# Quadrant moves of a transposed hidden tile, cut into four steps and a split and spread over the next pair of weight chunks

## The chip, the cores and the metric

The kernel runs on one core of one Trainium2 chip. The metric is the device time of one execution in microseconds (us), from start to end of the program on that core; lower is better. Three timed runs of the kernel before lie within 0.07% of each other.

## The reference, cut to what matters

A two-layer decoder trunk over 256 tokens of width 2048: attention, a SwiGLU feed-forward and a gated embedding in each layer. The change lies in the feed-forward:

```python
def swiglu(h, w1, w3, w2):
    return (jax.nn.silu(h @ w1) * (h @ w3)) @ w2      # D_MODEL = 2048, D_FF = 5632, SEQ = 256
```

Everything is float32.

## The kernel before, in words

**Products.** A float32 product is made of three TensorE products of a rounded format. Every operand is split into a high half (`hi`, a rounding copy on ScalarE, line 130 for weights and line 311 for activations) and a low half (`lo`, the difference, on VectorE, line 131 or 312). Lines 391, 392 and 393 multiply hi by hi, lo by hi and hi by lo into the same accumulator. All matmuls of the feed-forward are 128 x 128 by 128 x 512.

**Weight stream.** `WeightStream` loads blocks of four 128-row tiles by 512 columns (1 MB) from HBM, three raw buffers deep, and splits them up to three blocks ahead of their use, into three pairs of half buffers. A split therefore waits until TensorE has finished the block whose half buffer it takes over.

**A pair of chunks.** The hidden width is 11 chunks of 512 columns, in groups of 3, 4 and 4. For a chunk, `pair_of_chunks` makes the products with `w1` and `w3` together. The first four 128-row tiles of the contraction go through a seven-product form (Winograd's variant of Strassen), in which sums of weight tiles and of activation tiles are multiplied. Its small blocks live in three held tiles, `r11`, `r12` and `r2`; their halves `shi` and `slo` have a single buffer each, so a small split waits until TensorE is through with the small block before. In program order a pair is twelve blocks: small block 0 (`r11`, product `p1`, 6 matmuls), 1 (24 matmuls), small 2 (`r12`, `p7`, 6), 3 (24), small 4 (`r11`, `p5`, 6), 5 (24), 6 (`r2`, 12), 7 (24), small 8 (`r11`, `p6`, 6), 9 (24), small 10 (`r11`, 6), 11 (24): 186 matmuls. The weight sums (line 121) stand at the head of the split that reads them: block 2 first forms `r11 += r12` and `r12 += r2[1]`, block 8 `r11 += r2[1]`, block 10 `r11 += r2[0]`.

**End of a pair.** `feed_forward` takes the four accumulators, forms the hidden tile on VectorE and ScalarE (lines 619 to 626), and turns it with `transposed_blocks`: VectorE transposes 32 x 32 blocks (line 324), and sixteen moves of 32 x 256 elements on ScalarE (line 329) put each quadrant in its place. The result `xt` is split (lines 311 and 312) into `hid`, which is read only when the group's product with `w2` begins. All this is traced ahead of the next pair.

**Order.** The framework plans the order of each engine's instructions before the run: an instruction takes its place in its engine's queue by the planned time at which its inputs are ready, the earlier traced one first. On the chip each engine then works through its queue in that fixed order. `tc_order` adds an edge that only fixes the order of two instructions of one engine. `bg` is a list of deferred steps, and `work(n)` runs the next n of them at that place of the trace; the attention stages use it, the feed-forward does not.

Of the kernel before, what the change touches and what calls it, by code (L numbers as in the profile page):

```python
# [14 lines left out]
AF = mybir.ActivationFunctionType  # L15
# [23 lines left out]
CW = 512  # L39
# [4 lines left out]
SN = 2  # L44
# [19 lines left out]
def tc_order(tc, one, before):  # L64

    tc.add_manual_dep(one.ins, before.ins.name,
                      mybir.DependencyInfo(mybir.DependencyClass.NoSync, mybir.DependencyReason.DATA),
                      reason="order of one engine")
# [11 lines left out]
class WeightStream:  # L80
# [6 lines left out]
    def __init__(self, tc, raw_pool, half_pool, blocks):  # L87
        self.tc, self.nc, self.raw_pool, self.half_pool = tc, tc.nc, raw_pool, half_pool
        self.blocks = blocks
        self.held_pool = None  # L90
        self.loaded, self.halves, self.held = {}, {}, {}
        self.n_loaded = self.at = 0
        self.after = None

    def load(self, pool=None):
        i = self.n_loaded
# [18 lines left out]
    def split(self, i):  # L115
        while self.n_loaded <= i + self.LOAD and self.n_loaded < len(self.blocks):
            self.load()
        b = self.blocks[i]
        for o, p, j in b.sums:
            o, p = self.held[b.unit, o][:, 0, :], self.held[b.unit, p][:, j, :]  # L120
            self.nc.vector.tensor_add(o, o, p)  # L121
        raw = self.loaded.pop(i) if b.held is None else self.held[b.unit, b.held].rearrange("p a n -> p (a n)")
        if b.small:
            pool, width, bufs, tag = self.held_pool, SN * CW, 1, "s"
        else:
            pool, width, bufs, tag = self.half_pool, 4 * CW, None, ""
        hi = pool.tile([P, width], F32R, tag=tag + "hi", name=tag + "hi", bufs=bufs)
        lo = pool.tile([P, width], F32R, tag=tag + "lo", name=tag + "lo", bufs=bufs)
        m = b.a * b.n
        done = (self.nc.scalar.activation(hi[:, :m], raw[:, :m], AF.Copy),  # L130
                self.nc.vector.tensor_sub(lo[:, :m], raw[:, :m], hi[:, :m].bitcast(F32)))  # L131
        if self.after is not None:
            for one, before in zip(done, self.after):
                tc_order(self.tc, one, before)
        self.halves[i] = hi, lo
        return done

    def next(self):
# [17 lines left out]
def yoco_kernel(  # L156
# [5 lines left out]
    nc = tc.nc  # L162
# [16 lines left out]
    def pair_cols(wa, ca, wb, cb, nk):  # L179

        def at(w, k, c):
            return w[k * P:(k + SN) * P, c:c + CW].rearrange("(a p) n -> p a n", p=P)

        b11, b21, b12, b22 = at(wa, 0, ca), at(wa, SN, ca), at(wb, 0, cb), at(wb, SN, cb)
        rest = [cols(w, 2 * SN, nk - 2 * SN, c, CW) for w, c in ((wa, ca), (wb, cb))]
        def held(name, a=SN, **more):
            return Block(None, a, CW, held=name, unit=len(blocks), **more)

        return [held("r11", loads=[("r11", [b11])]), rest[0][0],
                held("r12", loads=[("r12", [b12]), ("r2", [b21, b22])], sums=[("r11", "r12", 0), ("r12", "r2", 1)]),  # L190
                rest[0][1], held("r11"), rest[1][0], held("r2", 2 * SN), rest[0][2],
                held("r11", sums=[("r11", "r2", 1)]), rest[1][1], held("r11", sums=[("r11", "r2", 0)]), rest[1][2]]

    IW = IDXN // 3
    FGROUPS = [(0, 3), (3, 7), (7, 11)]
# [118 lines left out]
            return (nc.scalar.activation(hi, src, AF.Copy, scale=gain),  # L314
                    nc.vector.scalar_tensor_tensor(lo, src, gain, hi.bitcast(F32), op0=ALU.mult, op1=ALU.subtract))

    def transposed_blocks(pool, src, out=None, bufs=1, moves=(0, 1)):


        xb = pool.tile([P, 4, 4, NT, 32], F32, tag="xb", name="xb", bufs=bufs)  # L320
        xt = (pool.tile([P, 4, S], F32, tag="xt", name="xt", bufs=1) if out is None else out).rearrange(
            "p k (t q) -> p k t q", t=NT)
        for t in range(NT):
            nc.vector.transpose(out=xb[:, :, :, t, :], in_=src[t].rearrange("p (k j f) -> p j k f", k=4, j=4))  # L324
        for i in range(4):
            for j in range(4):
                o, s = xt[32 * j:32 * j + 32, :, :, 32 * i:32 * i + 32], xb[32 * i:32 * i + 32, j]
                if moves[(i + j) % 2]:
                    nc.scalar.activation(o, s, AF.Copy)  # L329
                else:  # L330
                    nc.vector.tensor_copy(o, s)  # L331
        return xt.rearrange("p k t q -> p k (t q)")

    def x_to_station(st, g, c, pool=None, after=None, between=None):
# [44 lines left out]
    bg = deque()  # L379
# [78 lines left out]
    def pair_of_chunks(st, forms, nk, quad):  # L458


        c11, c21, c12, c22 = quad

        def tiles(k0, t):
            sl = slice(t * P, (t + 1) * P)
            return lambda j: (st[0][:, k0 + j, sl], st[1][:, k0 + j, sl])

        def form(o, of, alone, block=None, at=0):

            hi, lo, _ = stream.next() if block is None else block
            for j in range(SN):  # L470
                sl = slice((at + j) * CW, (at + j + 1) * CW)
                products_of(*of(j), o, hi[:, sl], lo[:, sl], alone in ("alone", "first") and j == 0,
                            alone in ("alone", "last") and j == SN - 1)

        def side_acc(i):
            if i < 2:
                return ps_at.tile([P, CW], F32, tag="at", name=f"side{i}")
            return ps_tr.tile([P, CW], F32, tag="tr", name=f"side{i}")

        ktiles = list(range(nk))  # L480
        p1, p5, p6, p7 = (side_acc(i) for i in (0, 2, 3, 1))
        v1, v6, v7, v8 = (forms.side(n) for n in ("v1", "v6", "v7", "v8"))
        form(p1, tiles(0, 0), "alone")
        nc.scalar.activation(v1, p1, AF.Copy)
        accumulate(st, ktiles, CW, (c11, c21), (), 2 * SN, 2 * SN + 4, new=(True, True))
        form(p7, forms.of(3), "alone")
        accumulate(st, ktiles, CW, (c11, c21), (), 2 * SN + 4, 2 * SN + 8)
        form(p5, forms.of(1), "alone")
        accumulate(st, ktiles, CW, (c12, c22), (), 2 * SN, 2 * SN + 4, new=(True, True))
        block = stream.next()  # L490
        form(c11, tiles(SN, 0), "more", block)
        form(c12, forms.of(4), "more", block, SN)
        accumulate(st, ktiles, CW, (c11, c21), (), 2 * SN + 8, stop=(True, False))
        form(p6, forms.of(2), "alone")
        nc.vector.tensor_add(v6, v1, p6)  # L495
        nc.vector.tensor_add(v7, v6, p7)
        nc.vector.tensor_sub(v6, v6, p5)
        nc.vector.tensor_sub(v8, v7, p5)
        accumulate(st, ktiles, CW, (c12, c22), (), 2 * SN + 4, 2 * SN + 8)
        form(c21, tiles(SN, 1), "last")  # L500
        return v1, v7, v6, v8
# [110 lines left out]
    def feed_forward(layer, st, forms, r, ss, nxt, scratch):  # L612
        for gi, (f0, f1) in enumerate(FGROUPS):
            hid = new_station()
            for f in range(f0, f1):
                quad = [ps_acc.tile([P, CW], F32, tag="acc", name=f"acc{j}") for j in range(4)]
                v = pair_of_chunks(st, forms, KT, quad)
                for t in range(NT):
                    nc.vector.tensor_add(v[t], v[t], quad[t])
                    sg = scratch.tile([P, CW], F32, tag="g", name="sg", bufs=1)  # L620
                    nc.scalar.activation(sg, v[t], AF.Sigmoid, scale=r[:, t:t + 1])  # L621
                    nc.vector.scalar_tensor_tensor(v[t], v[t], r[:, t:t + 1], sg, op0=ALU.mult, op1=ALU.mult)  # L622
                accumulate(st, ALL, CW, quad[2:], (), 2 * SN + 8)
                for t in range(NT):
                    nc.vector.tensor_sub(v[2 + t], quad[2 + t], v[2 + t])  # L625
                    nc.vector.scalar_tensor_tensor(v[2 + t], v[2 + t], r[:, t:t + 1], v[t], op0=ALU.mult, op1=ALU.mult)  # L626
                ut = transposed_blocks(scratch, v[2:], moves=(1, 1))
                sl = (slice(None), slice(4 * (f - f0), 4 * (f - f0) + 4), slice(None))
                split(hid[0][sl], hid[1][sl], ut)
            last = gi == len(FGROUPS) - 1  # L630
            for c in range(NC):
                acc = new_acc()
                accumulate(hid, list(range(4 * (f1 - f0))), CW, acc)
                for t in range(NT):
                    xs = x[t][:, c * CW:(c + 1) * CW]
                    nc.vector.tensor_add(xs, xs, acc[t])
                if last:
                    square_sum(ss, c, scratch)
                    nxt(c)
# [315 lines left out]
```

## Time and profile before

| what | value |
|---|---|
| time, median of 3 runs | 2231.34 us (2230.23 to 2231.75) |
| time of the profiled execution | 2229.82 us |
| its span, first to last instruction | 2228.0 us |
| TensorE matmul busy | 2178.8 us, 98% of the span |
| VectorE busy | 1627.3 us, 73% |
| ScalarE busy | 1315.1 us, 59% |
| mean granted TensorE clock | 0.999 |

The span is what the profile sees; the 1.8 us around it belong to the start and end of the program. Busy matmul time counts each record from its start to its modelled end, and consecutive ones overlap, so the space between two starts tells more than the length of one.

### The profile page before, as it was taken

Reading aid. Unit: us, or ns where it says so; the run is one execution under the profiler, and the core shown is the slowest. Engines: PE = TensorE matmul, PEld = TensorE weight load, DVE = VectorE, ACT = ScalarE, POOL = GpSimd, SP = SyncE. Lnnn points to the kernel's source line nnn. Section 1 sums busy time; section 2 is a strip of 40 time slices with the busy share of each in tenths; the row PEclk is TensorE's granted clock in tenths of the full one; section 3 lists DMA queues with packets and bytes.
Section 4 is the critical chain, followed back from the end, with each engine's and each line's share of the span. In section 5 each row is a group of like instructions: output and inputs, shape, how many; then the busy total and the mean of one; then the engine's idle time right before and its main releaser. Section 6 shows DMA issues by size and latency. Waiting matters only on the chain.

```text
span 2228.0 us, 24973 instructions
## 1 busy us (share of the span) xinstructions
PE 2178.8 (98%) x9780; PEld 1787.4 (80%) x9780; DVE 1627.3 (73%) x1706; ACT 1315.1 (59%) x1676; POOL 39.1 (2%) x38
## 2 busy tenths in 40 slices
PE   9999999999999999999999999999999999999998
PEld 8787787778778887788888778777877788778877
DVE  5777878866877478877777778787578756877764
ACT  5556676554675356666676657665356634666553
POOL 0121000000000000000000000000000000000000
PEclk9999999999999999999999999999999999999999
DMA  7554565656556555555566456556565566546553
GB/s 249 181 189 151 183 207 177 209 185 205 186 179 205 199 191 164 184 186 180 186 214 210 147 179 208 189 163 215 177 210 198 170 208 207 174 157 212 189 189 114
DMA packets 211382, 419.23 MB, mean 188 GB/s; under 512 B 7728, under 2 KB 14512, under 8 KB 211136
## 3 DMA queue, kind: packets, MB, share of 16 engines
q1 hardware_dynamic: 208400, 410.68, 55.3%
q0 software_dynamic: 1248, 4.27, 0.6%
q10 hardware_dynamic: 1616, 2.69, 0.3%
q8 instruction: 76, 1.25, 0.2%
q14 instruction: 42, 0.34, 0.0%
HBM read 415.48 MB, written 2.12 MB: 187 GB/s over the span
## 4 chain that ended last, share of the span: by engine, by line
PE 78%; ACT 10%; DVE 9%; issue 3%; DVEq 0%; POOLq 0%; POOL 0%; ACTq 0%
PE acc L393 23%; PE acc L392 23%; PE acc L391 23%; ACT xt L329 5%; DVE lo L131 2%; ACT hi L130 2%; PE side L391 2%; PE side L392 1%; PE side L393 1%; DVE v L626 1%; DVE v L622 1%; PE ps_s L553 1%; DVE slo L131 1%; DVE v L625 1%; PE ps_o L590 1%
## 5 line engine op out<-in xcount | busy, mean ns | idle before, releaser
L391 PE MATMUL acc<-hi,st_hi 128*128 128x512 f32 (+2 forms) x2828 | 1092.8, 387 | 3.3 <-ACT hi L130 3.3
L392 PE MATMUL acc<-lo,st_hi 128*128 128x512 f32 (+2 forms) x2828 | 1091.2, 386 | 2.7 <-DVE lo L131 2.6
L393 PE MATMUL acc<-hi,st_lo 128*128 128x512 f32 (+2 forms) x2828 | 1089.6, 386 | 0.0
L131 DVE TENSOR_TENSOR lo<-raw,hi 128x2048 fp32r<-128x2048 f32 (+1 forms) x347 | 794.6, 2291 | 324.0 <-ACT hi L130 321.4
L130 ACT ACTIVATE hi<-raw 128x2048 fp32r<-128x2048 f32 (+1 forms) x347 | 659.1, 1901 | 614.0 <-PE acc L393 516.3
L391 PEld LDWEIGHTS acc<-hi,st_hi 128*128 128x128 f32 x2828 | 530.7, 188 | 111.8 <-ACT hi L130 4.7
L392 PEld LDWEIGHTS acc<-lo,st_hi 128*128 128x128 f32 x2828 | 531.1, 188 | 110.5 <-DVE lo L131 6.1
L393 PEld LDWEIGHTS acc<-hi,st_lo 128*128 128x128 f32 x2828 | 530.9, 188 | 105.6 <-issue 2.0
L329 ACT ACTIVATE xt<-xb 32x256 f32<-32x256 f32 x544 | 226.2, 416 | 39.3 <-DVE xb L324 31.4
L131 DVE TENSOR_TENSOR slo<-r,shi 128x1024 fp32r<-128x1024 f32 x110 | 134.3, 1221 | 83.9 <-ACT shi L130 83.8
L130 ACT ACTIVATE shi<-r 128x1024 fp32r<-128x1024 f32 x110 | 115.7, 1052 | 71.0 <-DVE r L121 59.9
L121 DVE TENSOR_TENSOR r<-r,r 128x1024 f32<-128x1024 f32 x88 | 107.5, 1222 | 1.7
L391 PE MATMUL side<-shi,s_hi 128*128 128x512 f32 x132 | 54.3, 412 | 30.1 <-ACT shi L130 30.1
L131 DVE TENSOR_TENSOR lo<-r,hi 128x2048 fp32r<-128x2048 f32 x22 | 50.4, 2292 | 18.8 <-ACT hi L130 18.8
L391 PEld LDWEIGHTS side<-shi,s_hi 128*128 128x128 f32 x132 | 24.7, 187 | 45.0 <-ACT shi L130 41.1
L331 DVE COPY xt<-xb 32x256 f32<-32x256 f32 x192 | 54.5, 284 | 2.4
L495 DVE TENSOR_TENSOR v<-v,side 128x512 f32<-128x512 f32 x22 | 15.1, 686 | 56.2 <-PE side L393 56.2
L392 PE MATMUL side<-slo,s_hi 128*128 128x512 f32 x132 | 51.4, 389 | 0.0
L393 PE MATMUL side<-shi,s_lo 128*128 128x512 f32 x132 | 51.3, 389 | 0.0
L621 ACT ACTIVATE sg<-v,r_ffn 128x512 f32<-128x512 f32 x44 | 31.5, 717 | 31.4 <-DVE v L622 31.3
L130 ACT ACTIVATE hi<-r 128x2048 fp32r<-128x2048 f32 x22 | 41.9, 1905 | 12.0 <-PE acc L393 12.0
L567 ACT ACTIVATE sc<-sc,neg 128x128 f32<-128x128 f32 (+1 forms) x64 | 28.3, 444 | 31.2 <-DVE neg L565 31.2
(162 smaller groups left out, 1295.2 us busy)
## 6 DMA issues: line engine op xcount, KB each, us to landing
raw<-in_w_dram SPq DMA_DIRECT2D x220, 1024.0 KB, 5.2
r<-in_w_dram SPq DMA_DIRECT2D x88, 512.0 KB, 4.7
raw<-in_w_pg_dram SPq DMA_DIRECT2D x32, 1024.0 KB, 5.1
raw<-in_w_in_a_dram SPq DMA_DIRECT2D x24, 1024.0 KB, 5.2
raw<-in_w_out_a_dram SPq DMA_DIRECT2D x16, 1024.0 KB, 5.1
raw<-in_w_q_b_dram SPq DMA_DIRECT2D x16, 1024.0 KB, 5.1
raw<-in_w_out_b_dram SPq DMA_DIRECT2D x16, 1024.0 KB, 5.1
raw<-in_w_kv_dram SPq DMA_DIRECT2D x8, 1024.0 KB, 5.2
```

The costliest lines, as they stand in the source:

```text
L121: self.nc.vector.tensor_add(o, o, p)
L130: done = (self.nc.scalar.activation(hi[:, :m], raw[:, :m], AF.Copy), self.nc.vector.tensor_sub(lo[:, :m], raw[:, :m], hi[:, :m].bitcast(F32)))
L131: self.nc.vector.tensor_sub(lo[:, :m], raw[:, :m], hi[:, :m].bitcast(F32)))
L329: nc.scalar.activation(o, s, AF.Copy)
L331: nc.vector.tensor_copy(o, s)
L391: nc.tensor.matmul(o, sh, h, start=first, stop=False)
L392: nc.tensor.matmul(o, sh, l, start=False, stop=False)
L393: return nc.tensor.matmul(o, sl, h, start=False, stop=last)
L553: nc.tensor.matmul(o, qT[:, h0 + j, t * P:(t + 1) * P], self.kT[:, g, :nk], start=True, stop=True)
L567: nc.scalar.activation(sc[t][:, j, :], sc[t][:, j, :], AF.Exp, bias=neg[:, t, j:j + 1], accum_out=den[:, t, j:j + 1])
L590: nc.tensor.matmul(ps, self.v[s0][:, g * HD:(g + 1) * HD], pT[t + s0], start=(s0 == 0), stop=(s0 == t))
L621: nc.scalar.activation(sg, v[t], AF.Sigmoid, scale=r[:, t:t + 1])
```

## The change

The sixteen moves are no longer traced at the end of the pair. `transposed_blocks` hands back four steps of four moves, the split into `hid` is a fifth, and all five go into `bg`. The next pair runs them one at a time: behind its block 1, behind `p7`, behind block 3, behind `p5` and behind block 5. Each move is ordered behind the latest weight split on ScalarE. After the last pair of a group they run behind the first two blocks of the product with `w2`, three and two. The sums of the weights stand behind the split that last reads their tile before it is overwritten, and no longer ahead of the one that reads the sum. Each split is ordered behind the one before it, on ScalarE and on VectorE.

```diff
-        self.after = None
+        self.after = self.last = None
...
         b = self.blocks[i]
-        for o, p, j in b.sums:
-            o, p = self.held[b.unit, o][:, 0, :], self.held[b.unit, p][:, j, :]
-            self.nc.vector.tensor_add(o, o, p)
...
-        if self.after is not None:
-            for one, before in zip(done, self.after):
+        for start in (self.after, self.last):
+            for one, before in zip(done, start or ()):
                 tc_order(self.tc, one, before)
+        for o, p, j in b.sums:
+            o, p = self.held[b.unit, o][:, 0, :], self.held[b.unit, p][:, j, :]
+            self.nc.vector.tensor_add(o, o, p)
         self.halves[i] = hi, lo
+        self.last = done
...
-        return [held("r11", loads=[("r11", [b11])]), rest[0][0],
-                held("r12", loads=[("r12", [b12]), ("r2", [b21, b22])], sums=[("r11", "r12", 0), ("r12", "r2", 1)]),
-                rest[0][1], held("r11"), rest[1][0], held("r2", 2 * SN), rest[0][2],
-                held("r11", sums=[("r11", "r2", 1)]), rest[1][1], held("r11", sums=[("r11", "r2", 0)]), rest[1][2]]
+        return [held("r11", loads=[("r11", [b11])], sums=[("r11", "r12", 0), ("r12", "r2", 1)]), rest[0][0],
+                held("r12", loads=[("r12", [b12]), ("r2", [b21, b22])]), rest[0][1],
+                held("r11", sums=[("r11", "r2", 1)]), rest[1][0], held("r2", 2 * SN), rest[0][2],
+                held("r11", sums=[("r11", "r2", 0)]), rest[1][1], held("r11"), rest[1][2]]
...
-        for i in range(4):
+        def move(i):
             for j in range(4):
                 o, s = xt[32 * j:32 * j + 32, :, :, 32 * i:32 * i + 32], xb[32 * i:32 * i + 32, j]
                 if moves[(i + j) % 2]:
-                    nc.scalar.activation(o, s, AF.Copy)
+                    one = nc.scalar.activation(o, s, AF.Copy)
                 else:
                     nc.vector.tensor_copy(o, s)
+                if later is not None:
+                    tc_order(tc, one, stream.last[0])
+
+        for i in range(4):
+            if later is None:
+                move(i)
+            else:
+                later.append(lambda i=i: move(i))
...
-        accumulate(st, ktiles, CW, (c11, c21), (), 2 * SN, 2 * SN + 4, new=(True, True))
+        accumulate(st, ktiles, CW, (c11, c21), (1,), 2 * SN, 2 * SN + 4, new=(True, True))
         form(p7, forms.of(3), "alone")
-        accumulate(st, ktiles, CW, (c11, c21), (), 2 * SN + 4, 2 * SN + 8)
+        work(1)
+        accumulate(st, ktiles, CW, (c11, c21), (1,), 2 * SN + 4, 2 * SN + 8)
         form(p5, forms.of(1), "alone")
-        accumulate(st, ktiles, CW, (c12, c22), (), 2 * SN, 2 * SN + 4, new=(True, True))
+        work(1)
+        accumulate(st, ktiles, CW, (c12, c22), (1,), 2 * SN, 2 * SN + 4, new=(True, True))
...
-                ut = transposed_blocks(scratch, v[2:], moves=(1, 1))
+                later = []
+                ut = transposed_blocks(scratch, v[2:], moves=(1, 1), later=later)
                 sl = (slice(None), slice(4 * (f - f0), 4 * (f - f0) + 4), slice(None))
-                split(hid[0][sl], hid[1][sl], ut)
+                bg.extend(later)
+                bg.append(lambda ut=ut, sl=sl: split(hid[0][sl], hid[1][sl], ut))
...
-                accumulate(hid, list(range(4 * (f1 - f0))), CW, acc)
+                accumulate(hid, list(range(4 * (f1 - f0))), CW, acc, (3, 2) if c == 0 else ())
```

## Rows read from the trace of the kernel before

**Rows 1.** The page's head and its busy times, with shares and instructions.
```profile
span 2228.0 us, 24973 instructions
PE 2178.8 (98%) x9780; PEld 1787.4 (80%) x9780; DVE 1627.3 (73%) x1706; ACT 1315.1 (59%) x1676; POOL 39.1 (2%) x38
```

**Rows 2.** Waits of TensorE: total us, times, longest us.
```profile
PE side L391 <- ACT shi L130: 30.1, 18, 1.8
PE acc L391 <- ACT hi L130: 3.3, 2, 1.7
```

**Rows 3.** Windows, one period of a pair: us, busy PE, PEld, DVE, ACT, POOL, PEclk, DMA.
```profile
618.58:662.81 44.23, 42.52 (x186) 34.76 (x186) 36.15 (x32) 27.87 (x33) 0.00 (x0) 1.00 0.56 190
```

**Rows 4.** Timeline of TensorE from `p1` on: start, us, instruction, [idle before].
```profile
606.74 0.39 PE L391 MATMUL side<-shi,st_hi 128*128 128x512 f32 x1
...
607.42 0.39 PE L391 MATMUL side<-shi,st_hi 128*128 128x512 f32 x1
...
616.48 0.39 PE L392 MATMUL acc<-lo,st_hi 128*128 128x512 f32 x1
618.58 0.50 PE L391 MATMUL side<-shi,s_hi 128*128 128x512 f32 x1 [1.71 <-ACT shi L130]
618.92 0.40 PE L393 MATMUL acc<-hi,st_lo 128*128 128x512 f32 x1
...
620.07 0.39 PE L392 MATMUL side<-slo,s_hi 128*128 128x512 f32 x1
```

**Rows 5.** Timeline of ScalarE in the same stretch.
```profile
606.94 1.92 ACT L130 ACTIVATE hi<-raw 128x2048 fp32r<-128x2048 f32 x1 [1.12 <-PE acc L393]
608.80 0.60 ACT L484 ACTIVATE v<-side 128x512 f32<-128x512 f32 x1
610.62 6.83 ACT L329 ACTIVATE xt<-xb 32x256 f32<-32x256 f32 x16 [1.22 <-DVE xb L324]
617.47 1.06 ACT L130 ACTIVATE shi<-r 128x1024 fp32r<-128x1024 f32 x1
...
619.38 1.90 ACT L130 ACTIVATE hi<-r 128x2048 fp32r<-128x2048 f32 x1
```

**Rows 6.** Timeline of VectorE in the same stretch.
```profile
604.97 1.22 DVE L131 TENSOR_TENSOR slo<-r,shi 128x1024 fp32r<-128x1024 f32 x1
606.10 0.75 DVE L622 SCALAR_TENSOR_TENSOR v<-v,r_ffn,sg 128x512 f32<-128x512 f32 x1
...
609.28 1.31 DVE L324 STREAM_TRANSPOSE xb<-v 128x512 f32<-128x512 f32 x2
610.50 2.26 DVE L131 TENSOR_TENSOR lo<-raw,hi 128x2048 fp32r<-128x2048 f32 x1
612.67 2.48 DVE L121 TENSOR_TENSOR r<-r,r 128x1024 f32<-128x1024 f32 x2
618.56 1.23 DVE L131 TENSOR_TENSOR slo<-r,shi 128x1024 fp32r<-128x1024 f32 x1 [3.40 <-ACT shi L130]
```

**Rows 7.** Timeline of TensorE, first layer's first pair.
```profile
330.89 0.50 PE L391 MATMUL side<-shi,s_hi 128*128 128x512 f32 x1 [1.26 <-ACT shi L130]
```

**Rows 8.** Timeline of ScalarE at that place.
```profile
328.19 1.71 ACT L453 ACTIVATE xt<-xt,gT 128x256 f32<-128x256 f32 x4
```

**Rows 9.** Timeline of TensorE, product with `w2` after the group of three.
```profile
463.68 0.39 PE L393 MATMUL acc<-hi,st_lo 128*128 128x512 f32 x1
465.73 0.73 PE L391 MATMUL acc<-hi,st_hi 128*128 128x512 f32 x2 [1.66 <-ACT hi L130]
```

**Rows 10.** Timeline of ScalarE at that place.
```profile
453.22 1.92 ACT L130 ACTIVATE hi<-raw 128x2048 fp32r<-128x2048 f32 x1 [1.12 <-PE acc L393]
456.91 6.83 ACT L329 ACTIVATE xt<-xb 32x256 f32<-32x256 f32 x16 [1.76 <-DVE xb L324]
```

**Rows 11.** Timeline of the SP queue: issues of the held tiles' loads.
```profile
575.58 0.37 SPq L105 DMA_DIRECT2D r<-in_w_dram  x1
...
587.57 0.88 SPq L105 DMA_DIRECT2D r<-in_w_dram  x2
```

More of the change, by code (lines that the diff above doesn't have):

```diff
@@ L315, in split, with transposed_blocks @@
                     nc.vector.scalar_tensor_tensor(lo, src, gain, hi.bitcast(F32), op0=ALU.mult, op1=ALU.subtract))
-    def transposed_blocks(pool, src, out=None, bufs=1, moves=(0, 1)):
+    def transposed_blocks(pool, src, out=None, bufs=1, moves=(0, 1), later=None):
         xb = pool.tile([P, 4, 4, NT, 32], F32, tag="xb", name="xb", bufs=bufs)
```

## The prediction

> **What bounds the kernel now.** I read the page's busy times first: matmuls fill 2178.8 of 2228.0 us, the other engines 73% and 59% at most [rows 1]. So only time in which TensorE stands still can be won. Next the waits of TensorE alone: almost all are one kind, the first product of a small block waiting for its `shi`, 18 times and 30.1 us, and two waits of a plain block for `hi`, 3.3 us [rows 2]. Then one whole period of a pair: 44.23 us for 186 matmuls, VectorE busy 36.15, ScalarE 27.87, granted clock 1.00 [rows 3]. Last the three engines in the same 16 us.
>
> TensorE: three matmuls take 607.42 - 606.74 = 0.68 us, so one takes 0.227. `p7`, which should follow block 1, starts at 618.58, 2.10 us after the matmul before it, and the next follows after 0.34 [rows 4]. Lost are 2.10 - 0.227 = 1.87 and 0.34 - 0.227 = 0.11, together 1.98 us. Check: 186 x 0.227 = 42.2, and the period is 44.23 [rows 3], 2.0 more.
>
> ScalarE: that `shi` of `r12` starts at 617.47, straight behind sixteen moves that took 6.83 us from 610.62 [rows 5]. Its own inputs, the sums, were there at about 615.1 on VectorE, which then idled 3.40 us for the `shi` [rows 6]. So ScalarE's queue is what is late, by work that nobody needs for many microseconds: `hid` is read only in the product with `w2`.
>
> How often: of the 18 waits two belong to the first pairs of the layers, 1.26 us of idle each [rows 7], where no hidden tile is turned yet; ahead of the `shi` stand the four scalings of line 453 [rows 8]. That leaves (30.1 - 2.5) / 16 = 1.72 us each, as in [rows 4]. The sixteen are the pairs that follow another pair in their group, 2 + 3 + 3 in each layer. The two waits for `hi` stand in the product with `w2` after the group of three, where sixteen moves from 456.91 to 463.74 hold up the `hi` of a block that TensorE wants after 463.68 [rows 9, 10].
>
> **The moves.** The same sixteen instructions remain, 0.427 us each (6.83 / 16), and nothing is removed. The order edge puts the first four behind the `shi` of `r12`, the next four behind `hi` of block 6, and so on. I take `p1` at 606.74 as zero hour and follow the new queues.
>
> ScalarE: `hi` of block 5 and the copy of `p1` end at 609.4 [rows 5]. `shi` of `r12` can follow at once if its sums are done, and `p1` has freed the buffer by then (6 x 0.227 = 1.36 us after 606.74). It would be ready at 609.4 + 1.05 = 610.5; TensorE ends block 1 at 608.10 + 24 x 0.227 = 613.5. So `p7`'s first product no longer waits: minus 1.98 us.
>
> **The sums.** Two of 1.22 us move ahead of the hidden tile's last steps. On VectorE they become ready when `slo` of `r11` ends, at 606.1; line 622 is traced earlier and goes first, the sums then run from about 606.8 to 609.2. Everything behind them comes 2.45 us later: transposes end at 613.0 in place of 610.6, `lo` of block 5 at 615.1, `slo` of `r12` at 616.3 [rows 6]. No VectorE work is added, only the 3.40 us of idle go. `p7`'s second product needs that `slo`; it stands 0.227 us after the first, at 613.8. So a new wait of 616.3 - 613.8 = 2.6 us is possible. What hides it is block 3, whose halves were ready before: the old queue ran products of block 3 ahead of `p7` (that at 616.48 is one) and five more between `p7`'s first at 618.58 and its second at 620.07, and that second one waited for nothing although its `slo` had ended only at 619.8 [rows 4, 6]. I expect some eleven products (2.5 us) of block 3 there. The cost lies between 0 and 2.6 us a pair; I take 0, because the old filling at the same place fitted.
>
> The loads of `r12` and `r2` are issued 29 and 17 us before `slo` of `r11` runs [rows 6, 11], so the sums wait for no data in a steady pair. The tile `r2` comes free one split sooner, so its load can only come earlier on SP's queue.
>
> **The next tight place, `p5`.** `p7` would end near 617.5. ScalarE by then: four moves 613.0 to 614.8, `hi` of block 6 to 616.6, four moves to 618.3, `shi` of block 4 to 619.4. VectorE: `slo` of `r12` to 616.3, `lo` of block 6 616.7 to 618.9, `slo` of block 4 to 620.5. TensorE ends block 3 at 613.5 + 30 x 0.227 = 620.3 and wants that `slo` at 620.6. It fits by 0.1 us, without room: four moves late by a tenth each would be a wait. I charge 0.15 us a pair, between 0 and 0.6. Later steps have room: `hi` of block 7 is done by 623.0, the last moves by 624.7, the split of `hid` by 625.7, and TensorE wants block 7 at 606.74 + 23.1 = 629.8.
>
> **Splits in sequence.** The old queue of ScalarE already runs them in the traced order (blocks 5, 2, 6 in [rows 5]): nothing changes, 0.
>
> **The product with `w2`.** It starts when the pair's last block ends, about 0.2 us ahead of the `hi` at 453.22 which waited for that, and a block takes 24 x 0.227 = 5.44 us [rows 10]. The moves could start 456.91 + 2.45 - 453.0 = 6.3 us in; a `hi` of 1.9 goes between, ready at 5.6, so they run from 7.5 to 14.3, and the split's halves are there at 15.3 and 16.6. After a group of four the last tile is wanted 3 x 5.44 = 16.3 us in, its low half 0.45 us later: no wait. After the group of three it is wanted at 10.9, and is not there. Today's loss there is 465.73 - 463.68 - 0.227 = 1.8 us and 0.11 after it [rows 9]. The queue has to be filled with the next column's block and was planned for moves shorter than they are; all sixteen still precede the split. I expect the loss to stay, with bounds of 0 and 1.9 for each layer. The first pairs' 1.5 us stay too; the diff leaves those scalings alone.
>
> **The sum.** Minus 16 x 1.98 = 31.7, plus 16 x 0.15 = 2.4: minus 29.3 us. The profiled execution took 2229.82 us (span 2228.0 and 1.8 around it), so 2200.5 by its own time. The median of the runs is 1.5 us above it: 2202.0.
>
> **The rivals.** *The wait comes back smaller*: `p5` or `p7` waits 0.6 us to 1.3 us in each of the sixteen pairs, since ScalarE's moves stand between the splits. For it speaks the margin of 0.1 us; against it that products of block 3 and 5 can fill. Time: 2231.3 - 31.7 + 16 x 0.95 = 2215.
>
> *VectorE takes ScalarE's place* (the other side): the sums hold up `lo` of block 5 and with it `slo` of `r12`, and TensorE's queue has `p7`'s second product right behind its first. Then each pair waits 2.6 us where it lost 1.98: 16 x 0.6 = 10 us slower, 2241. It decides from the point at which fewer than three products of block 3 stand between the two. For it speaks VectorE's share, 36.15 of 44.23 us; against it that the plan knows VectorE's order. The Trainium skill says that VectorE and ScalarE work off their queues strictly first in, first out (TensorE: Matmul & The Clock Gate, Architectural detail); this trace agrees, the `shi` at 617.47 stands behind the moves although its input was there at 615.1. By that rule the sums, once placed ahead, delay all that follows, which is this rival.
>
> *Nothing is won*: the queue plan puts something else ahead of the `shi` of `r12`, such as the sums late, behind `lo` of block 5 (done at 615.1 as now), and TensorE's gap stays. `shi` would then be ready at 616.2, in time for `p7`'s old place at 616.7, so even then the loss goes; for no change the plan would have to draw `p7` ahead by two microseconds as well. About 2231.
>
> *More is won*: the two waits in the product with `w2` go as well, 2 x 1.9: 2231.3 - 31.7 - 3.9 = 2195.7.
>
> **How the numbers follow.** My forecast (2198 to 2208) 0.6; smaller wait back 0.17; all won 0.1; nothing 0.05; VectorE late 0.08. A change within 0.2% (4.5 us) is about what a measurement of this kernel cannot tell from none. Faster by more: 0.6 + 0.17 + 0.1 and a little of the others' spread, 0.88; same 0.05; slower 0.07. The range runs from the case that all is won and no pair pays anything, 2194, to the smaller wait at its upper half, 2217; beyond stand the last two rivals.
>
> **What would show it.** In the changed kernel's waits of TensorE the 18 waits for `shi` shrink to the two of the first pairs. A pair's period is 42.2 to 42.4 us in place of 44.23. On ScalarE `shi` of `r12` runs right behind the copy of `p1`, with the sixteen moves in four groups among splits; on VectorE the sums stand between lines 622 and 625. About eleven products of block 3 stand inside `p7`. The prediction is wrong if TensorE's waits name `slo` at `p7` or `p5`, or if the product with `w2` waits longer than 1.9 us.

## The result and the profile after

The changed kernel takes 2212.03 us (median of 4 runs, 2210.84 to 2214.19), the kernel before 2231.39 (4 runs): ratio 0.9915, 95% interval 0.9898 to 0.9932. It is 19.4 us faster where 29.3 were forecast; 2212 lies in the stated range and near the 2215 of the rival in which a smaller wait comes back.

The page's head and busy times:

```profile
span 2209.1 us, 24961 instructions
PE 2177.4 (99%) x9780; PEld 1788.8 (81%) x9780; DVE 1629.6 (74%) x1706; ACT 1313.7 (59%) x1676; POOL 39.1 (2%) x38
```

The work of the engines is that of [rows 1]; the 18.9 us are idle time of TensorE. Its waits (total us, times, longest us):

```profile
PE side L401 <- DVE slo L128: 9.9, 16, 0.6
PE acc L400 <- ACT st_hi L312: 4.1, 2, 2.0
PE side L400 <- ACT shi L127: 2.5, 2, 1.3
...
PE acc L401 <- DVE lo L128: 1.7, 5, 0.5
```

Lines 400 to 402 are the old 391 to 393. Of the 18 waits for `shi` in [rows 2] the two of the first pairs are left. In place of the other sixteen stand sixteen shorter ones, for a `slo`. One period of a pair, in the view of windows:

```profile
603.48:646.60 43.12, 42.50 (x188) 34.83 (x187) 36.12 (x32) 27.82 (x32) 0.00 (x0) 1.00 0.57 197
```

It was 44.23 us [rows 3]: 1.11 us less, 16 times, makes 17.8. The other 1.1 us are the net of smaller things. The waits for `lo` fell from 2.6 to 1.7 us (at 1339 us of the kernel before, one product waited 0.91 us); the two waits in the product with `w2` grew from 3.3 [rows 2] to 4.1 us; the remainder was not followed. The line of the kernel before:

```profile
PE acc L392 <- DVE lo L131: 2.6, 6, 0.9
```

The timeline of TensorE in that pair, `p7` and then `p5`:

```profile
610.28 0.39 PE L400 MATMUL side<-shi,s_hi 128*128 128x512 f32 x1
...
613.22 0.39 PE L401 MATMUL side<-slo,s_hi 128*128 128x512 f32 x1
...
617.08 0.39 PE L400 MATMUL side<-shi,s_hi 128*128 128x512 f32 x1
618.09 0.50 PE L401 MATMUL side<-slo,s_hi 128*128 128x512 f32 x1 [0.62 <-DVE slo L128]
618.43 0.40 PE L402 MATMUL side<-shi,s_lo 128*128 128x512 f32 x1
```

`p7` waits for nothing, with (613.22 - 610.28) / 0.227 = 13 places, so twelve other products, between its first and second. `p5`'s second product comes 1.01 us behind its first, and the next 0.34 after it: 0.78 + 0.11 = 0.9 us lost. ScalarE there:

```profile
606.63 1.06 ACT L127 ACTIVATE shi<-r 128x1024 fp32r<-128x1024 f32 x1 [1.03 <-DMA raw<-in_w_dram]
...
610.48 1.92 ACT L127 ACTIVATE hi<-r 128x2048 fp32r<-128x2048 f32 x1 [2.30 <-PE acc L402]
612.30 3.39 ACT L330 ACTIVATE xt<-xb 32x256 f32<-32x256 f32 x8
615.72 1.06 ACT L127 ACTIVATE shi<-r 128x1024 fp32r<-128x1024 f32 x1
```

The `shi` of `r12` stands ahead of the moves. Eight moves in one piece stand ahead of the `shi` of block 4, which `p7` would have let start at 614.6 (its last product starts at 614.13, and in the kernel with four moves ahead the same `shi` starts 0.43 us behind that product). VectorE there:

```profile
603.50 1.22 DVE L134 TENSOR_TENSOR r<-r,r 128x1024 f32<-128x1024 f32 x1
...
605.24 1.22 DVE L134 TENSOR_TENSOR r<-r,r 128x1024 f32<-128x1024 f32 x1
...
608.89 2.29 DVE L128 TENSOR_TENSOR lo<-raw,hi 128x2048 fp32r<-128x2048 f32 x1
611.09 0.71 DVE L325 STREAM_TRANSPOSE xb<-v 128x512 f32<-128x512 f32 x1
611.72 1.18 DVE L128 TENSOR_TENSOR slo<-r,shi 128x1024 fp32r<-128x1024 f32 x1
...
616.81 1.22 DVE L128 TENSOR_TENSOR slo<-r,shi 128x1024 fp32r<-128x1024 f32 x1 [1.70 <-ACT shi L127]
```

VectorE idled 1.70 us for that `shi`. It is the engine that the wait names, and it is not the one that is late.

### The profile page after: what moved, and what is told of

Read it like the earlier page. It is cut to its first block, busy times and chain, and to the rows that moved or that the text cites. A ratio compares the mean times of both kernels' runs of the same rounds, so it can differ in the third digit from the quotient of the medians.

```text
span 2209.1 us, 24961 instructions
## 1 busy us (share of the span) xinstructions
PE 2177.4 (99%) x9780; PEld 1788.8 (81%) x9780; DVE 1629.6 (74%) x1706; ACT 1313.7 (59%) x1676; POOL 39.1 (2%) x38
## 3 DMA queue, kind: packets, MB, share of 16 engines
q8 instruction: 76, 1.25, 0.2%
## 4 chain that ended last, share of the span: by engine, by line
PE 85%; ACT 7%; DVE 5%; issue 2%; DMA 0%; POOLq 0%; POOL 0%; DVEq 0%; ACTq 0%
PE acc L401 26%; PE acc L402 26%; PE acc L400 26%; ACT xt L330 3%; ACT hi L127 3%; DVE lo L128 2%; PE side L401 2%; PE side L402 1%; PE side L400 1%; PE ps_s L564 1%; PE ps_o L601 1%; DVE slo L128 1%; ACT shi L127 1%; DVE xt L332 1%; PE ps_p L592 0%
## 5 line engine op out<-in xcount | busy, mean ns | idle before, releaser
L649 DVE TENSOR_TENSOR x<-x,acc 128x512 f32<-128x512 f32 x48 | 32.8, 688 | 14.4 <-PE acc L402 14.4
```

## The experiments

The theory: TensorE's queue was planned with moves shorter than they are on the chip (0.42 us), so TensorE waits where enough of them stand ahead of a split that it wants soon. The rivals: the sums won the time; VectorE is late; the moves are simply too much work in that place. A loss per pair is the period less 42.16 us, the period of the kernels in which no pair waits.

**Sums alone.** The kernel before, with the sums behind the split, all sixteen moves in one piece.

```diff
         b = self.blocks[i]
-        for o, p, j in b.sums:
-            o, p = self.held[b.unit, o][:, 0, :], self.held[b.unit, p][:, j, :]
-            self.nc.vector.tensor_add(o, o, p)
...
                 tc_order(self.tc, one, before)
+        for o, p, j in b.sums:
+            o, p = self.held[b.unit, o][:, 0, :], self.held[b.unit, p][:, j, :]
+            self.nc.vector.tensor_add(o, o, p)
...
```

The list of blocks, left out here, names each sum at the split that it now follows.

> The kernel before with only the weight sums moved behind the split they wait for; the sixteen moves stay in one piece. In this queue the shi of r12 stands ahead of the moves, and all sixteen stand ahead of the shi of block 4 (p5). Theory (the queue was planned with moves about 0.1 us shorter than they are, so TensorE waits about 0.11 us for each move that stands ahead of a small split): the wait goes from p7 to p5 and keeps its size, 1.8 to 1.9 us in each of the sixteen pairs, the period stays near 44.1 us and the time is 2226 to 2231 us. Rival (the sums won the 19 us, since they free the shi of r12): 2212 us. Rival (the moves are simply too much work in that place, and what the plan thought does not matter): eight more moves than in the changed kernel are 3.4 us more, a wait of 4.3 us a pair, 2260 us.

Measured: 2233.88 us, ratio 1.0014 (1.0005 to 1.0024), 2.9 us above the expected range. The rival of the sums falls, and so does that of too much work. A period is 44.35 us, a loss of 2.19 where 1.8 to 1.9 was expected. ScalarE's timeline, TensorE's, and the period:

```profile
615.16 6.80 ACT L329 ACTIVATE xt<-xb 32x256 f32<-32x256 f32 x16
621.98 1.06 ACT L127 ACTIVATE shi<-r 128x1024 fp32r<-128x1024 f32 x1
```

```profile
623.09 0.50 PE L391 MATMUL side<-shi,s_hi 128*128 128x512 f32 x1 [1.86 <-ACT shi L127]
```

```profile
578.74:623.09 44.35, 42.50 (x186) 34.83 (x186) 35.84 (x32) 27.70 (x33) 0.00 (x0) 1.00 0.56 190
```

The wait has gone from `p7` to `p5` and about kept its size (2.07 before). Eight moves more than in the changed kernel take 6.80 - 3.39 = 3.4 us, but cost 1.2 us more: TensorE's queue has ten products of block 5 ahead of `p5`'s second one (five ahead of its first and five behind that), 2.27 us. So the plan had allowed for some 0.28 us a move, and 0.14 us a move were missing. This is an estimate: a queue can only be filled by whole products.

**Twelve ahead.**

```diff
-        accumulate(st, ktiles, CW, (c11, c21), (1,), 2 * SN, 2 * SN + 4, new=(True, True))
+        accumulate(st, ktiles, CW, (c11, c21), (2,), 2 * SN, 2 * SN + 4, new=(True, True))
...
-        accumulate(st, ktiles, CW, (c12, c22), (1,), 2 * SN, 2 * SN + 4, new=(True, True))
+        accumulate(st, ktiles, CW, (c12, c22), (0,), 2 * SN, 2 * SN + 4, new=(True, True))
```

> The changed kernel with twelve moves, three steps, ahead of the shi of block 4 in place of eight. TensorE's queue now holds four products of block 3 between p5's first and second. Theory (moves longer than planned): the twelve end 1.70 us later than the eight, the queue allows for 0.91 of them, so p5 loses 0.9 + 0.8 = 1.7 us a pair and the time is 2222 to 2227 us. Rival (work in that place, nothing planned for): 0.9 + 1.7 = 2.6 us a pair, 2239 us. Rival (p5's wait is VectorE's, which is behind with its slo, and not ScalarE's): no change, 2212 us.

(The four products are of block 5; 0.91 us for four moves, 0.23 each.) Measured: 2224.71 us, ratio 0.9972 (0.9962 to 0.9983), as the theory had it. ScalarE, and the period: a loss of 1.74 us.

```profile
615.54 5.09 ACT L330 ACTIVATE xt<-xb 32x256 f32<-32x256 f32 x12
620.66 1.06 ACT L127 ACTIVATE shi<-r 128x1024 fp32r<-128x1024 f32 x1
```

```profile
577.87:621.77 43.90, 42.61 (x187) 34.77 (x187) 36.02 (x32) 27.70 (x33) 0.00 (x0) 1.00 0.56 192
```

**Four ahead.**

```diff
         form(p7, forms.of(3), "alone")
-        work(1)
-        accumulate(st, ktiles, CW, (c11, c21), (1,), 2 * SN + 4, 2 * SN + 8)
+        work(0)
+        accumulate(st, ktiles, CW, (c11, c21), (2,), 2 * SN + 4, 2 * SN + 8)
```

> The changed kernel with the second step of four moves behind the shi of block 4: four moves ahead of it, twelve behind. The queues of TensorE and VectorE are the same instruction for instruction as in the changed kernel; only ScalarE's differs. Theory (ScalarE's moves are late there): the eight moves end at 615.7 in the changed kernel and p7 lets the small buffer go at 614.5, so with four moves less the shi starts 1.1 us sooner, its slo is there before TensorE wants it, the 16 x 0.9 = 14.4 us go, 2197.6 us. Rival (VectorE is what is late): p5 waits as before, 2212 us.

Measured: 2196.66 us, ratio 0.9847 (0.9832 to 0.9861). ScalarE:

```profile
609.48 1.68 ACT L330 ACTIVATE xt<-xb 32x256 f32<-32x256 f32 x4
611.74 1.06 ACT L127 ACTIVATE shi<-r 128x1024 fp32r<-128x1024 f32 x1 [0.58 <-PE side L402]
```

ScalarE now waits for `p7`, and of the waits of `side` only the two of the first pairs remain. The traces hold VectorE's and TensorE's instructions in the same order as in the changed kernel, so with their queues untouched the wait for VectorE's `slo` is gone: it was ScalarE's. Four moves cost nothing, since the `shi` is held by `p7` until they are done.

**None ahead.**

```diff
-        accumulate(st, ktiles, CW, (c11, c21), (1,), 2 * SN, 2 * SN + 4, new=(True, True))
+        accumulate(st, ktiles, CW, (c11, c21), (0,), 2 * SN, 2 * SN + 4, new=(True, True))
         form(p7, forms.of(3), "alone")
-        work(1)
-        accumulate(st, ktiles, CW, (c11, c21), (1,), 2 * SN + 4, 2 * SN + 8)
+        work(0)
+        accumulate(st, ktiles, CW, (c11, c21), (2,), 2 * SN + 4, 2 * SN + 8)
...
-        accumulate(st, ktiles, CW, (c12, c22), (1,), 2 * SN, 2 * SN + 4, new=(True, True))
+        accumulate(st, ktiles, CW, (c12, c22), (2,), 2 * SN, 2 * SN + 4, new=(True, True))
```

> The changed kernel with no move ahead of the shi of block 4: eight behind it, four behind the hi of block 7, four and the hidden split behind block 5. TensorE's and VectorE's queues are the same instruction for instruction as in the changed kernel. Theory: p5 waits for nothing, a period of 42.2 us, 2197 to 2199 us, the same as with four ahead, because the shi is then held only by p7. Rival (the moves only push the wait on, to the hi of block 7 or the shi of block 8): a part of the 14.4 us comes back there, over 2202 us. Rival (VectorE is late): 2212 us.

Measured: 2196.82 us, ratio 0.9848 (0.9833 to 0.9862), the same as with four. Nothing comes back later, though eight moves now stand in one piece behind block 7's `hi`. The period is TensorE's own work, with no idle time:

```profile
1614.86:1657.02 42.16, 42.16 (x187) 34.92 (x186) 35.92 (x32) 27.60 (x32) 0.00 (x0) 1.00 0.59 201
```

So the loss a pair is 0, 0, 0.96, 1.74 and 2.19 us with 0, 4, 8, 12 and 16 moves ahead of `p5`'s split. (The sixteen are those of the kernel before with its sums moved.) It grows with the moves but not in proportion: some room takes up the first ones, and TensorE's queue puts more products ahead when more moves are planned.

**The moves alone.** The sums back at the head of the split that reads them, and the list of blocks, left out here, as in the kernel before.

```diff
         b = self.blocks[i]
+        for o, p, j in b.sums:
+            o, p = self.held[b.unit, o][:, 0, :], self.held[b.unit, p][:, j, :]
+            self.nc.vector.tensor_add(o, o, p)
...
-        for o, p, j in b.sums:
-            o, p = self.held[b.unit, o][:, 0, :], self.held[b.unit, p][:, j, :]
-            self.nc.vector.tensor_add(o, o, p)
...
```

> The changed kernel with the weight sums back at the head of the split that reads them; the moves stay in four steps and in sequence. Theory (only how many moves stand ahead of a small split counts): the sums, late again behind lo of block 5, hold the shi of r12 to about 616 us on the old clock, and TensorE's queue fills with thirteen products of block 3 until then, which costs nothing; eight moves still stand ahead of the shi of block 4, so p5 loses about 0.9 us a pair as in the changed kernel: 2210 to 2216 us. Rival (the sums' new place won the time): the loss of 1.98 us a pair is back, 2228 to 2232 us.

Measured: 2217.24 us, ratio 0.9937 (0.9922 to 0.9951), 1.2 us above the expected range. The period is 43.41 us, a loss of 1.25:

```profile
578.26:621.67 43.41, 42.70 (x187) 34.64 (x187) 36.19 (x32) 27.65 (x33) 0.00 (x0) 1.00 0.57 194
```

Most of the gain comes from the moves. With late sums the `shi` of `r12` is late too (ScalarE stands idle 5.83 us for the sums ahead of it) and so is all that follows on ScalarE; `p5` then already waits for its `shi`. The sums' new place, worth nothing alone, is worth 2217.2 - 2212.0 = 5 us on top of the moves, 16 x 0.29.

**No sequence.**

```diff
-        for start in (self.after, self.last):
+        for start in (self.after,):
```

> The changed kernel without the edges that keep the splits in sequence. Inside a pair ScalarE's and VectorE's queues stay the same; only at the ends of the groups does a small split come earlier. Theory (the edges are worth nothing in the pairs): 2212 us, within 1.5. Rival (the edges help, or harm, in the pairs): a change of 16 times some tenths of a us, over 3 us.

Measured: 2211.27 us, ratio 0.9911 (0.9895 to 0.9928); the changed kernel's own is 0.9915. The edges are worth nothing that can be told in the time. The traces show two effects at the ends of the groups that about cancel. Without the edges TensorE runs three products of the next pair's `p1` ahead of its wait in the product with `w2`, and the two waits there are 1.4 us each in place of 2.0; but one wait of 0.92 us for a `lo` is back at 1330 us.

**A fuller queue.** The moves stay where the change puts them; TensorE is told to run six products of block 5 first. (`form` and `accumulate` hand back their products for this; that part is left out.)

```diff
...
-        form(p5, forms.of(1), "alone")
+        ahead = []
+        five = form(p5, forms.of(1), "alone")
         work(1)
-        accumulate(st, ktiles, CW, (c12, c22), (1,), 2 * SN, 2 * SN + 4, new=(True, True))
+        accumulate(st, ktiles, CW, (c12, c22), (1,), 2 * SN, 2 * SN + 4, new=(True, True), into=ahead)
+        tc_order(tc, five[1], ahead[5])
```

> The changed kernel with one more edge on TensorE: p5's second product stands behind the sixth product of block 5. The eight moves stay ahead of the shi of block 4, and ScalarE's order inside a pair is that of the changed kernel. Theory (the wait is one of queue order: TensorE has other products that are ready, but was not told that the shi would be late): six products fill 1.36 us, more than the 0.9 us lost, and 2196 to 2199 us come out although ScalarE is as late as before. Rival (ScalarE's and VectorE's work in that place is simply too much, and a wait filled there comes back at the next split): over 2205 us.

Measured: 2196.9 us, ratio 0.9847 (0.9832 to 0.9861). ScalarE and TensorE:

```profile
612.01 3.39 ACT L330 ACTIVATE xt<-xb 32x256 f32<-32x256 f32 x8
615.43 1.06 ACT L127 ACTIVATE shi<-r 128x1024 fp32r<-128x1024 f32 x1
```

```profile
616.79 0.39 PE L400 MATMUL side<-shi,s_hi 128*128 128x512 f32 x1
...
618.38 0.39 PE L401 MATMUL side<-slo,s_hi 128*128 128x512 f32 x1
```

The `shi` is as late as in the changed kernel, 1.36 us ahead of `p5`'s first product in both, and TensorE waits for nothing there. ScalarE's and VectorE's instructions stand in the same order as in the changed kernel; only TensorE's differ. This is what tells the theory from plain overload: what was missing was an order that knew how late the `shi` would be.

**Half of the moves on VectorE** in the last pair of a group of three, on top of none ahead, whose lines are left out here.

```diff
-                    nc.vector.tensor_copy(o, s)
+                    one = nc.vector.tensor_copy(o, s)
                 if later is not None:
-                    tc_order(tc, one, stream.last[0])
+                    tc_order(tc, one, stream.last[0 if moves[(i + j) % 2] else 1])
...
-                ut = transposed_blocks(scratch, v[2:], moves=(1, 1), later=later)
+                ut = transposed_blocks(scratch, v[2:], moves=(0, 1) if f == 2 else (1, 1), later=later)
```

> The kernel with no move ahead of the shi of block 4, and in the last pair of each group of three half of the sixteen moves on VectorE. Theory (in the product with w2 after that group TensorE waits 2.2 us for the hidden tile because sixteen moves on one engine come later than planned): with eight on each engine the wait falls to 1 us or less in each of the two layers, 2 to 3 us faster than with none ahead alone, 2194 to 2195 us. Rival (the wait there is set by the splits and not by the moves): 2197 us.

Measured: 2193.14 us, ratio 0.983 (0.9816 to 0.9845), the fastest of all, and 0.9 us faster than expected. Its wait for the hidden tile:

```profile
PE acc L400 <- ACT st_hi L312: 1.6, 2, 0.8
```

4.1 us of idle became 1.6, so 2.5 of the 3.7 us gained over none ahead. Where the rest comes from is in the last section.

## Why the prediction was right in part

**Right.** That the sixteen waits at `p7` are ScalarE's queue and go; that the first pairs' waits stay (2.5 us before and after); that the sums, though they delay the transposes, cost nothing at `p7`, because products of block 3 fill it (eleven were expected, twelve stand there); that sequence, in the net, costs and brings nothing. The rival in which VectorE takes ScalarE's place did not happen: `p7`'s second product runs at 613.22, straight behind the twelve.

**By its own signs** the prediction is wrong in two places: TensorE's waits name `slo` at `p5`, and the wait in the product with `w2` is 2.03 us, longer than 1.9. The time is not in the forecast's 2198 to 2208, which had a chance of 0.6. What came is the rival *The wait comes back smaller*, with a chance of 0.17, and in its size: it had charged 16 x 0.95, and 16 x 0.96 was measured. That 2212 lies within the stated range is due to this rival and not to the sum.

**The step that failed** is "The next tight place, `p5`": the place was right, the charge of 0.15 us a pair was not. It measured 0.96 as a loss of the period, outside its own bounds of 0 to 0.6. On the new clock (`p1` at 603.48, so 3.26 us less) I had the `shi` of block 4 at 615.0 and its `slo` done at 617.2; they came at 615.7 and 618.0. The order that I wrote down was wrong in one point: the second transpose runs behind `lo` of block 5, ends at 611.8 and not at 609.7, so block 6's `hi` goes first and the eight moves behind it in one piece. ScalarE's same work, some 5.3 us, then starts at 610.48 and not at 609.7. That is 0.7 us, against a margin of 0.1. I had seen that the plan counts the moves too short, at the group of three, and did not apply it at `p5`, where eight of them stand ahead of a split.

**The sum by measured terms.** A pair lost 44.23 - 42.16 = 2.07 us before (I had 1.98) and loses 0.96 now: 16 x 1.11 = 17.8, and 1.1 from outside the pairs, which was not foreseen and is only in part traced: 18.9, as between the spans. From the forecast of 29.3 that is 16 x (0.96 - 0.15) = 13.0 less at `p5`, 16 x 0.09 = 1.4 more for the old loss, and the 1.1.

**The product with `w2`.** The loss after the group of three stayed, as forecast, but it grew over its bound of 1.9: TensorE now stands still for 2.03 us there, where [rows 9] had 1.66. Again sixteen moves precede the split, and the edges that keep the splits in sequence have a part in it, since without them it is 1.4. TensorE, and ScalarE:

```profile
464.10 0.50 PE L400 MATMUL acc<-hi,st_hi 128*128 128x512 f32 x1 [2.03 <-ACT st_hi L312]
```

```profile
454.18 5.12 ACT L330 ACTIVATE xt<-xb 32x256 f32<-32x256 f32 x12 [1.50 <-DVE xb L325]
...
461.26 1.69 ACT L330 ACTIVATE xt<-xb 32x256 f32<-32x256 f32 x4
462.99 1.06 ACT L312 ACTIVATE st_hi<-xt 128x1024 fp32r<-128x1024 f32 x1
```

The kernel with half of the moves on VectorE, 0.8 us, shows that the moves set most of this wait. What the plan takes for a move was not read off directly; it is worked out from the products that its queue puts ahead.

## What to carry to other kernels

Where an order is planned ahead and an engine keeps to it, a wait tells that the plan misjudged a duration: find the instruction that is longer than planned, and keep it from standing ahead of work that TensorE wants soon, or give TensorE other work that is ready to run first. Spreading such instructions is not enough by itself; count how many stand ahead of each split with little room, since four cost nothing here, eight about half of the old loss and sixteen all of it. The engine that a wait names can be a victim too: look at what it idled for itself.

## What the runs showed of the hardware that was not expected

After a wait of TensorE, most often the one in the product with `w2`, its granted clock fell in some executions to half for 3.4 us. In the profiled execution of the kernel with none ahead it happened once, in the first layer (windows: stretch, busy by engine, clock, DMA):

```profile
463.00:466.40 3.40, 3.40 (x9) 2.62 (x9) 2.29 (x1) 0.53 (x1) 0.00 (x0) 0.50 0.77 295
466.40:472.00 5.60, 5.60 (x26) 4.58 (x26) 1.77 (x3) 1.92 (x1) 0.00 (x0) 1.00 0.57 187
```

That is the lower of the two levels, 1.2 GHz of 2.4; nine products start where a stretch of equal length in the kernel with half of the moves on VectorE has sixteen:

```profile
461.00:464.40 3.40, 3.40 (x16) 2.65 (x15) 2.82 (x2) 1.42 (x1) 0.00 (x0) 1.00 0.67 258
```

Ahead of the fall TensorE had stood still for 2.03 us, up to 461.77; in the other kernel it was 0.79 us, and the clock stayed. Half the clock for 3.4 us costs 1.7 us, which is more than the 1.2 us that the kernel with half of the moves gained beyond its shorter waits.

The other profiled executions agree. Four more kernels (the moves alone, twelve ahead, four ahead, the fuller queue) show one fall each, behind the same wait of 2.03 us. The sums alone show two, at 841.32 and 1500.09 us, each behind a wait of 1.86 or 1.87 us at `p5`, so 3.4 us of its time are the clock; but its fastest execution, 2232.65 us, is above the expected range too, as the larger loss a pair has it. The kernel before, the changed one, the one without sequence and the one with half of the moves show none. The mean granted clock of an execution counts the falls: it is 0.999 in every profile without one, 0.998 with one and 0.997 with two. By that reading the fastest executions of four ahead and of the fuller queue, at 0.999, have no fall; they take 2195.7 us, and half of the moves 2193.1, also at 0.999. That is 2.6 us, about the 2.5 by which the waits are shorter, so the rest of the gain was the clock.

The changed kernel had the same 2.03 us twice and kept its clock, so such a wait can be followed by the fall and need not be; what decides was not settled.
